# A two-layer decoder trunk: all of x loaded ahead of the weights, the first chunk reordered, the norms' transposes moved, and a bank of its own for the last 256 columns

## The chip, the cores and the metric

The kernel runs on one core of one Trainium2 chip. The metric is the device time of one execution in microseconds (us). Engine names are those of the profile: PE multiplies matrices, PEld is its weight load, DVE and ACT work element by element, POOL is a further element engine that also issues some DMAs, SP issues most DMAs. A number behind an `L` is a line of the kernel's source.

## The reference, cut to what matters

The trunk has two layers on 256 tokens of width 1024. Each layer is a half-step feed-forward network, a token mixer, and another half-step feed-forward network, each behind an RMS norm; a last RMS norm ends it.

```python
def rms_norm(x, w):
    y = xf * lax.rsqrt(jnp.mean(xf * xf, axis=-1, keepdims=True) + EPS)
    return (y * w)
def swiglu(x, w_in, w_out):
    gate, up = jnp.split(x @ w_in, 2, axis=-1)
    return (jax.nn.silu(gate) * up) @ w_out

for l in range(2):
    h = h + 0.5 * swiglu(rms_norm(h, ffn1_norm[l]), ffn1_w_in[l], ffn1_w_out[l])
    u = rms_norm(h, mix_norm[l])
    ... = jnp.split(u @ w_in[l], split_points, axis=-1)
    y_s = mamba2_branch(...); y_d = deltanet_branch(...)
    merged = sigmoid(gate_s) * (y_s @ ssm_w_branch[l]) + sigmoid(gate_d) * (y_d @ dn_w_branch[l])
    h = h + merged @ w_out[l]
    h = h + 0.5 * swiglu(rms_norm(h, ffn2_norm[l]), ffn2_w_in[l], ffn2_w_out[l])
return rms_norm(h, final_norm)
```

All inputs are float32.

## The kernel before

**Tiles and precision.** The 256 tokens are two token tiles of 128 (`t` = 0, 1). The stream `h` stays in SBUF as 128 x 2 x 1024. The weights come as a stream of 128 x 1024 tiles (`wraw`, 512 KB each), loaded by SP in the order of use (`load`, L157), five at a time. `prep` (L173) splits each into a high half `whi` (ACT, L67) and a low half `wlo` (DVE, L70); up to five split tiles exist. Activations are split in the same way, and each product is three matmuls: high x high, high x low weight, low x high (`mm3`, L315).

**Order of issue.** The program is written in one order, and a scheduler orders each engine's instructions from that; `tc.issue_after(ins)` puts an instruction behind another one, and `tc.high_priority` puts some ahead. Per tile index, `state["behind"]` names instructions that a split goes behind, and `state["late"]` one that only its low half goes behind. `take` (L201) hands the next split tile to a chunk and issues loads and splits ahead of it.

**Norms.** `norm_in` (L288) works tile by tile. For a token tile, `rstd_of` (L260) takes two square sums of 512 columns on ACT (`junk`), adds them on DVE (`zz`, L78), and takes the power of minus one half on POOL (`rsqrt`, L208). `rms_chain` (L271) then multiplies on DVE (`hn`, two halves of 512 columns), transposes each half on PE with four 128 x 128 transposes into a bank `hnT` (L281), and splits the bank into `uW`, high by ACT and low by DVE. There are five such norms between stages, and a sixth at the start, where `h` is x itself and the norm vector is spread by two matmuls from one row (`nw`, L245).

**The first chunk behind a norm.** `tok_chunk` (L329) multiplies four weight tiles (two 128-row slices each) by token tile 0, 24 matmuls of 512 columns, and then by token tile 1. PE does tile 0 while the norm of tile 1 is still under way on ACT, DVE and POOL; the transposes of tile 1 stand after 18 matmuls, with one matmul between their two groups. In a feed-forward network the next chunks are `fc` (`chan_chunk`, L346); in the mixer they are `z` chunks, and the mixer's small weights `wsr` are loaded, split into `wsc` (L561 to 564), and used behind the second `z` chunk.

**Start.** SP issues the norm row, token tile 0 of x, the identity (part of `cs`), four weight tiles, then token tile 1 of x (L221 to 230).

**End.** The last chunk of the last feed-forward network (`out_chunks` with `split`, L366) ends with 15 matmuls of 512 columns for token tile 1. `add` (L389) puts them on `h`, and L1248 to 1258 take the last norm, scale two halves of 512 columns, and SP issues two output DMAs per token tile.

## Time and profile before

| | us |
|---|---|
| median of 3 runs (lowest, highest) | 1547.75 (1547.63, 1549.64) |
| the profiled execution's own time | 1548.12 |
| its span, first instruction to last | 1546.4 |
| PE busy in the span | 1525.9 |
| DVE, ACT, POOL busy | 1228.8, 949.3, 86.9 |

A row of the timeline reads: start in us, duration in us, engine, line, operation, what is written `<-` what is read, the matmul's array shape, shape and type, the number of instructions merged; in brackets the idle time of the engine ahead of it and what ended it. A row of the waits reads: engine and what it waited with `<-` what it waited for, us in total, times, longest. A row of the windows reads: from:to, length, busy us and instructions of PE, PEld, DVE, ACT and POOL, PEclk, DMA busy share, GB/s. The end of a matmul is modelled: a 512-column matmul is shown with 0.39 us, while in an unbroken run the next one starts 0.23 us after it.

### The profile page before, as it was taken

Reading aid. Unit: us, or ns where it says so; the run is one execution under the profiler, and the core shown is the slowest. Engines: PE = TensorE matmul, PEld = TensorE weight load, DVE = VectorE, ACT = ScalarE, POOL = GpSimd, SP = SyncE. Lnnn points to the kernel's source line nnn. Section 1 sums busy time; section 2 is a strip of 40 time slices with the busy share of each in tenths; the row PEclk is TensorE's granted clock in tenths of the full one; section 3 lists DMA queues with packets and bytes.
Section 4 is the critical chain, followed back from the end, with each engine's and each line's share of the span. In section 5 each row is a group of like instructions: output and inputs, shape, how many; then the busy total and the mean of one; then the engine's idle time right before and its main releaser. Section 6 shows DMA issues by size and latency. Waiting matters only on the chain.

```text
span 1546.4 us, 29049 instructions
## 1 busy us (share of the span) xinstructions
PE 1525.9 (99%) x11458; PEld 1383.8 (89%) x11458; DVE 1228.8 (79%) x1856; ACT 949.3 (61%) x1534; POOL 86.9 (6%) x92
## 2 busy tenths in 40 slices
PE   8999999999999999999999999999999999999998
PEld 7999879999888888999899998899998888889996
DVE  6878769967899766788778887789579996678886
ACT  5655667765665645565555566676756665455564
POOL 0000110000000000000100012010000000000010
PEclk9999999999999999999999999999999999999999
DMA  7677765553465455577866687565345555556775
GB/s 273 193 265 228 226 223 169 185 164 110 177 209 172 158 170 192 185 248 214 266 220 226 204 253 236 183 196 184 117 138 203 178 168 184 177 178 190 248 240 156
DMA packets 98831, 305.73 MB, mean 198 GB/s; under 512 B 22837, under 2 KB 23813, under 8 KB 97670
## 3 DMA queue, kind: packets, MB, share of 16 engines
q1 hardware_dynamic: 94086, 291.29, 55.9%
q0 software_dynamic: 4608, 12.58, 4.9%
q8 instruction: 90, 1.47, 0.4%
q14 instruction: 47, 0.39, 0.1%
HBM read 297.72 MB, written 1.92 MB: 194 GB/s over the span
## 4 chain that ended last, share of the span: by engine, by line
PE 86%; DVE 5%; issue 3%; ACT 3%; DMA 2%; POOL 1%; POOLq 0%; SPq 0%; ACTq 0%; DVEq 0%
PE fc L327 9%; PE fc L321 9%; PE fc L326 9%; PE o L318 3%; PE o L317 3%; PE o L316 3%; PE t L316 3%; PE t L317 3%; PE t L318 3%; PE b L318 3%; PE b L316 3%; PE b L317 3%; PE p L317 2%; PE p L316 2%; PE p L318 2%
## 5 line engine op out<-in xcount | busy, mean ns | idle before, releaser
L70 DVE TENSOR_TENSOR wlo<-wraw,whi 128x1024 fp32r<-128x1024 f32 x488 | 592.2, 1221 | 188.1 <-ACT whi L67 174.5
L67 ACT ACTIVATE whi<-wraw 128x1024 fp32r<-128x1024 f32 x488 | 511.6, 1059 | 268.1 <-PE fc L326 91.6
L327 PE MATMUL fc<-uW,wlo 128*128 128x256 f32 x1280 | 354.8, 277 | 0.0
L321 PE MATMUL fc<-uW,whi 128*128 128x256 f32 x1280 | 354.0, 277 | 0.0
L326 PE MATMUL fc<-uW,whi 128*128 128x256 f32 x1260 | 348.2, 276 | 0.0
L321 PEld LDWEIGHTS fc<-uW,whi 128*128 128x128 f32 x1280 | 240.4, 188 | 0.8
L327 PEld LDWEIGHTS fc<-uW,wlo 128*128 128x128 f32 x1280 | 240.6, 188 | 0.0
L326 PEld LDWEIGHTS fc<-uW,whi 128*128 128x128 f32 x1260 | 236.5, 188 | 0.8
L67 ACT ACTIVATE whi<-wsum 128x1024 fp32r<-128x1024 f32 x64 | 68.0, 1062 | 58.8 <-PE fc L326 32.7
L316 PE MATMUL t<-whi,uW 128*128 128x512 f32 x256 | 101.9, 399 | 0.0
L317 PE MATMUL t<-wlo,uW 128*128 128x512 f32 x256 | 100.9, 394 | 0.2 <-DVE wlo L70 0.2
L318 PE MATMUL t<-whi,uW 128*128 128x512 f32 x256 | 100.5, 392 | 0.0
L70 DVE TENSOR_TENSOR wlo<-wsum,whi 128x1024 fp32r<-128x1024 f32 x64 | 78.2, 1222 | 7.9 <-ACT whi L67 5.6
L316 PE MATMUL b<-whi,bh 128*128 128x512 f32 x192 | 76.1, 398 | 0.3 <-ACT bh L67 0.2
L317 PE MATMUL b<-wlo,bh 128*128 128x512 f32 x192 | 74.9, 390 | 0.0
L318 PE MATMUL b<-whi,bl 128*128 128x512 f32 x192 | 74.3, 394 | 0.3 <-DVE bl L70 0.3
L321 PE MATMUL xs<-uW,whi 128*128 128x256 f32 x256 | 72.8, 285 | 0.0
L327 PE MATMUL xs<-uW,wlo 128*128 128x256 f32 x256 | 71.4, 279 | 0.0
L326 PE MATMUL xs<-uW,whi 128*128 128x256 f32 x254 | 70.6, 278 | 0.0
L316 PE MATMUL o<-whi,gh 128*128 128x512 f32 x160 | 62.5, 391 | 0.0
L318 PE MATMUL o<-whi,gl 128*128 128x512 f32 x160 | 62.3, 389 | 0.0
L317 PE MATMUL o<-wlo,gh 128*128 128x512 f32 x160 | 62.3, 389 | 0.0
(332 smaller groups left out, 3401.3 us busy)
## 6 DMA issues: line engine op xcount, KB each, us to landing
wraw<-in_wst_dram SPq DMA_DIRECT2D x504, 512.0 KB, 5.0
wsum<-in_wst_dram SPq DMA_DIRECT2D x16, 512.0 KB, 7.0
wsum<-in_wst_dram POOLq DMA_DIRECT2D x16, 512.0 KB, 8.2
dc<-rdram SPq DMA_DIRECT2D x8, 1024.0 KB, 8.1
nw<-in_norms_dram SPq DMA_DIRECT2D x6, 512.0 KB, 7.5
h<-u POOLq DMA_DIRECT2D x12, 256.0 KB, 6.3
gb<-rdram SPq DMA_DIRECT2D x8, 256.0 KB, 6.0
h<-in_x_dram SPq DMA_DIRECT2D x4, 256.0 KB, 5.6
```

The lines of the kernel that those rows point to most:

```text
L67: return A.activation(out=o, in_=i, func=func, **kw)
L70: return V.tensor_tensor(out=o, in0=a, in1=b, op=op)
L316: PE.matmul(ps, lh, rh, start=start, stop=False)
L317: PE.matmul(ps, lh, rl, start=False, stop=False)
L318: return PE.matmul(ps, ll, rh, start=False, stop=stop)
L321: PE.matmul(ps, wh, mh, start=start, stop=False)
L326: PE.matmul(ps, wh, ml, start=False, stop=False)
L327: PE.matmul(ps, wl, mh, start=False, stop=stop)
```

## The change

- **x first.** SP issues all four DMAs of x ahead of the weights. The norm row and the identity are issued by ACT.
- **First norm and first chunk** (`norm_first`, new). The norm chains of both token tiles come ahead of the first weight split's low half; only the first bank of each tile is transposed ahead of the chunk, the second banks after 9 and 12 of its matmuls as written. `tok_chunk` takes each weight tile for both token tiles before the next one.
- **The five norms.** For token tile 1 the transposes are written into `tok_chunk` after matmuls 18 and 20 (`TURN`); the low half of tile n+3 goes behind the `hn` of tile 1, the split of n+4 behind its transposes; the last two slices of token tile 0 are multiplied high x high, low x high, then high x low weight.
- **The mixer's small weights.** The split of `wsc` is written behind the first `z` chunk.
- **The end.** For token tile 1 the last 512 columns are multiplied as twice 256, the second 256 into a bank of their own (`tail`); the square sums, the addition and the product with the norm vector follow these pieces; the last output DMA is issued by ACT.

```diff
+TURN = (17, 19)
...
-        ahead("prepped", min(j + 1 if state["hold"] else j + NSPL, n_forms), prep)
+        ahead("prepped", min(j + 1 if state["hold"] else j + NSPL, n_forms, state["cap"]), prep)
...
-    nc.sync.dma_start(row[:], norms[0:1, :])
+    nc.scalar.dma_start(row[:], norms[0:1, :])
+    nc.scalar.dma_start(cs[:, 0:P], cst[:, 0:P])
     for t in range(2):
         for n in range(2):
             nc.sync.dma_start(
                 h[:, t, n * 512 : (n + 1) * 512], x[t * P : (t + 1) * P, n * 512 : (n + 1) * 512]
             )
-        if t == 0:
-            nc.sync.dma_start(cs[:, 0:P], cst[:, 0:P])
-            ahead("loaded", 4, load)
+    ahead("loaded", 4, load)
...
+    def norm_first(nw):
+
+        place_input()
+        with tc.high_priority(offset=PRI):
+            _, turn0 = rms_chain(0, nw)
+            ins, turn1 = rms_chain(1, nw)
+            state["behind"][0], state["late"][0] = [state["square"].ins], ins
+            ahead("prepped", 1, prep)
+            with tc.issue_after(state["whi"].ins):
+                first = turn0(0)
+            with tc.issue_after(first[0].ins):
+                done = turn1(0)
+        for i in range(1, 4):
+            state["behind"][i] = [done[0].ins]
+            state["late"][i] = done[1]
+        state["turns"] = {8: (turn0, 1), 11: (turn1, 1)}
+        state["first_chunk"] = True
...
                 state["behind"][n + 4] = (state["square"].ins, ins.ins)
                 state["late"][n + 2] = added
-                state["input"] = done
+                state["late"][n + 3] = ins
+                state["turns"] = {i: (turn, n_) for n_, i in enumerate(TURN)}
+                state["cap"] = n + 4
...
+        order = [(t, k0, w) for t in range(2) for k0, w in ws]
+        if first:
+            order.sort(key=lambda o: o[1])
+        i = 0
+        for t, k0, (wh, wl) in order:
+            three = []
+            for k in range(2):
+                uh, ul = (u[:, k0 + k, t * P : (t + 1) * P] for u in (uTh, uTl))
+                high, low = (w[:, k * 512 : (k + 1) * 512] for w in (wh, wl))
+                three.append([(uh, high), (uh, low), (ul, high)])
+            if t == 0 and len(ws) == 4 and k0 == (0 if first else KT - 2):
+                three = [[m[j] for m in three] for j in ((0, 1, 2) if first else (0, 2, 1))]
+            three = sum(three, [])
+            for j, (st, mv) in enumerate(three):
+                ins = PE.matmul(ps[t][:], st, mv, start=k0 == 0 and j == 0, stop=k0 == KT - 2 and j == 5)
+                if i in state["turns"]:
+                    turn, n = state["turns"].pop(i)
+                    with tc.high_priority(offset=PRI), tc.issue_after(ins.ins):
+                        state["input"] = turn(n)
+                    if not state["turns"] and state["cap"] < n_forms:
+                        state["late"][state["cap"]] = state["input"][1]
+                        state["cap"] = n_forms
+                i += 1
...
+                if t == 1 and split:
+                    order = [o for o in order if o[1] == 0]
+                    order += [(k, 1, c, c + 256) for c in (0, 256) for k in range(len(kk))]
...
+                    if c0:
+                        begin, bank = k == kk[0], ps[2][:, 0:256]
...
+            if nw is None and t == 1:
+                banks.append((po[2][:, 0:256], 768))
...
         z_unit(0, None)
-
+        wsc = cpool.tile([P, KT, 2, 48], F32R, tag="wsc", name="wsc")
+        with tc.issue_after(state["input"][0].ins), tc.issue_after(state["input"][1].ins):
+            act(wsc[:, :, 0], wsr[:])
+            tt(wsc[:, :, 1], wsr[:], f(wsc[:, :, 0]), ALU.subtract)
...
+        cuts = ((0, 512), (512, 1024)) if t == 0 else ((0, 512), (512, 768), (768, 1024))
...
+        nc.sync.dma_start(out[t * P : (t + 1) * P, 0:512], o[0][:])
+        (nc.scalar if t else nc.sync).dma_start(out[t * P : (t + 1) * P, 512:1024], o[1][:])
```

What the change moves on the engines, at three places.

ACT at the start, before, from the second square sum of token tile 0 on; `uW_108` is the transposed input, of token tile 0 in the first pair and of tile 1 in the second, `hnT_...` the four banks, `junk` the square sums:

```order
L67 ACTIVATE junk_112,ss_109<-h_78 128x512
L67 ACTIVATE whi_135<-wraw_85 128x1024
L67 ACTIVATE uW_108<-hnT_121 128x4x128
L67 ACTIVATE uW_108<-hnT_128 128x4x128
L67 ACTIVATE whi_139<-wraw_87 128x1024
L67 ACTIVATE whi_193<-wraw_89 128x1024
L67 ACTIVATE junk_144,ss_143<-h_78 128x512
L67 ACTIVATE junk_146,ss_143<-h_78 128x512
L67 ACTIVATE whi_197<-wraw_91 128x1024
L67 ACTIVATE uW_108<-hnT_155 128x4x128
L67 ACTIVATE uW_108<-hnT_162 128x4x128
```

and with the change, where the first two `uW` rows are the first banks of tile 0 and tile 1, and the later two the second banks:

```order
L68 ACTIVATE junk_112,ss_109<-h_78 128x512
L68 ACTIVATE junk_122,ss_121<-h_78 128x512
L68 ACTIVATE junk_124,ss_121<-h_78 128x512
L68 ACTIVATE whi_133<-wraw_87 128x1024
L68 ACTIVATE uW_108<-hnT_137 128x4x128
L68 ACTIVATE uW_108<-hnT_144 128x4x128
L68 ACTIVATE whi_175<-wraw_89 128x1024
L68 ACTIVATE whi_179<-wraw_91 128x1024
L68 ACTIVATE whi_183<-wraw_93 128x1024
L68 ACTIVATE uW_108<-hnT_218 128x4x128
L68 ACTIVATE whi_187<-wraw_165 128x1024
L68 ACTIVATE uW_108<-hnT_228 128x4x128
```

The square sums of tile 1 moved ahead of the first weight split, and the last bank of tile 1 now stands behind the split of the fifth weight tile (`whi_187`).

DVE at the second norm, before, from the square sums of token tile 1 (`zz_6809`) to the end of its input; `wlo_6851` is the low half of tile n+3 and `wlo_6855` that of n+4:

```order
L78 TENSOR_SCALAR zz_6809<-ss_6804 128x1
L70 TENSOR_TENSOR wlo_6851<-wraw_6692,whi_6850 128x1024
L73 SCALAR_TENSOR_TENSOR hn_6812<-h_78,zz_6809,nw_2185 128x512
L73 SCALAR_TENSOR_TENSOR hn_6814<-h_78,zz_6809,nw_2185 128x512
L70 TENSOR_TENSOR wlo_6855<-wraw_6694,whi_6854 128x1024
L70 TENSOR_TENSOR uW_108<-hnT_6816,uW_108 128x4x128
L70 TENSOR_TENSOR uW_108<-hnT_6823,uW_108 128x4x128
```

and with the change:

```order
L79 TENSOR_SCALAR zz_6809<-ss_6804 128x1
L74 SCALAR_TENSOR_TENSOR hn_6812<-h_78,zz_6809,nw_2171 128x512
L74 SCALAR_TENSOR_TENSOR hn_6814<-h_78,zz_6809,nw_2171 128x512
L71 TENSOR_TENSOR wlo_6837<-wraw_6692,whi_6836 128x1024
L71 TENSOR_TENSOR uW_108<-hnT_6864,uW_108 128x4x128
L71 TENSOR_TENSOR uW_108<-hnT_6873,uW_108 128x4x128
L71 TENSOR_TENSOR wlo_6919<-wraw_6694,whi_6918 128x1024
```

Each of the two low halves moved back by one step: n+3 behind `hn`, n+4 behind `uW`.

ACT in the first mixer, before, from the input of token tile 1 on; `yz` is the output of the first `z` chunk for a token tile, `whi_2215` the split of tile n+5, the second tile of the next chunk:

```order
L67 ACTIVATE uW_108<-hnT_2178 128x4x128
L67 ACT_TABLE_LOAD
L67 ACTIVATE ea_2379<-rp_2189 128x40
L67 ACT_TABLE_LOAD
L67 ACTIVATE yz_2196<-t0_2197 128x512
L67 ACTIVATE wsc_2193<-wsr_2191 128x8x48
L67 ACTIVATE whi_2215<-wraw_2051 128x1024
L67 ACTIVATE whi_2221<-wraw_2053 128x1024
```

and with the change, where `whi_2304` is the same split:

```order
L68 ACTIVATE uW_108<-hnT_2225 128x4x128
L68 ACTIVATE yz_2179<-t0_2180 128x512
L68 ACTIVATE whi_2304<-wraw_2051 128x1024
L68 ACTIVATE wsc_2262<-wsr_2177 128x8x48
L68 ACTIVATE whi_2308<-wraw_2053 128x1024
L68 ACT_TABLE_LOAD
L68 ACTIVATE ea_2379<-rp_2175 128x40
L68 ACTIVATE whi_2312<-wraw_2055 128x1024
L68 ACT_TABLE_LOAD
```

The split of tile n+5 moved ahead of `wsc`, and the two table loads with `ea` behind it.

More of the change, by code (lines that the diff above doesn't have):

```diff
@@ L147, in trunk_kernel @@
     n_forms = len(plan)
-    state = {"loaded": 0, "prepped": 0, "taken": 0, "last": None, "hold": False, "behind": {}, "late": {}, "first": 0}
+    state = {"loaded": 0, "prepped": 0, "taken": 0, "last": None, "hold": False, "behind": {}, "late": {}, "first": 0, "turns": {}, "first_chunk": False, "cap": n_forms}
     raws, halves = {}, {}
@@ L560, in mixer @@
             nc.sync.dma_start(wsr[:], wsm[l])
-        wsc = cpool.tile([P, KT, 2, 48], F32R, tag="wsc", name="wsc")
-        with tc.issue_after(state["input"][0].ins), tc.issue_after(state["input"][1].ins):
-            act(wsc[:, :, 0], wsr[:])
-            tt(wsc[:, :, 1], wsr[:], f(wsc[:, :, 0]), ALU.subtract)
         snw = lp[:, 240:256]
```

93 lines of the change are left out of this document (43 added, 50 removed).

## Prediction

> **What bounds the kernel now.** I read the busy shares first, then PE's waits, then PE's stretch at each place that the diff touches.
>
> ```profile
> PE 1525.9 (99%) x11458; PEld 1383.8 (89%) x11458; DVE 1228.8 (79%) x1856; ACT 949.3 (61%) x1534; POOL 86.9 (6%) x92
> ...
> PE hnT L281 <- DVE hn L73: 3.6, 7, 0.9
> PE cbb L1006 <- DVE vb L70: 2.9, 2, 1.6
> ...
> PE t L317 <- DVE wlo L70: 0.2, 1, 0.2
> ```
>
> PE, the matmul engine, is busy 99% of the span, and no matmul is taken away. So only time in which PE stands still can be won: at the start, at the five norms between stages, at the end. The wait rows (us in total, times, longest) put the largest group there: the transposes `hnT` wait seven times for `hn`, twice at the start and once at each of the five norms. The waits inside the mixers (`cbb` and others) are not touched; they are for chains that start from PE's own earlier products and so move with PE. What PE gains at one of these places therefore arrives at the end.
>
> **The five norms.** Token tile 0 is normalised while PE is still at the stage before. Tile 1 is normalised while PE multiplies tile 0. The rows are those of the second norm; first DVE and POOL for tile 0, then the same chain for tile 1, then PE.
>
> ```profile
> 592.22 0.21 DVE L78 TENSOR_SCALAR zz<-ss 128x1 f32<-128x1 f32 x1 [0.79 <-ACT junk L67]
> 592.51 0.56 POOL L209 TENSOR_TENSOR zz<-zz,mhalf 128x1 f32<-128x1 f32 x1 [61.43 <-DVE zz L78]
> 593.10 1.41 DVE L73 SCALAR_TENSOR_TENSOR hn<-h,zz,nw 128x512 f32<-128x512 f32 x2 [0.67 <-POOL zz L209]
> ...
> 600.24 0.21 DVE L78 TENSOR_SCALAR zz<-ss 128x1 f32<-128x1 f32 x1
> 600.36 1.21 DVE L70 TENSOR_TENSOR wlo<-wraw,whi 128x1024 fp32r<-128x1024 f32 x1
> 600.52 1.47 POOL L209 TENSOR_TENSOR zz<-zz,mhalf 128x1 f32<-128x1 f32 x1 [7.45 <-DVE zz L78]
> 602.03 1.41 DVE L73 SCALAR_TENSOR_TENSOR hn<-h,zz,nw 128x512 f32<-128x512 f32 x2 [0.46 <-POOL zz L209]
> ...
> 602.15 0.39 PE L318 MATMUL f<-whi,uW 128*128 128x512 f32 x1
> 602.93 0.63 PE L281 MATMUL hnT<-cs,hn 128*128 128x128 f32 x4 [0.39 <-DVE hn L73]
> ...
> 186.18 0.40 PE L318 MATMUL o<-whi,gl 128*128 128x512 f32 x1
> 186.42 1.04 PE L281 MATMUL hnT<-cs,hn 128*128 128x128 f32 x8
> ```
>
> From `zz` to `hn` it is 0.88 us for tile 0 and 1.79 us for tile 1. The difference is the power on POOL: 0.56 us alone, 1.47 us while DVE runs a weight split (`wlo`) beside it. The change puts that split behind `hn`, so I expect 0.88 us again: `hn` at 601.12 instead of 602.03, its first half by 601.87. PE reaches the transposes 0.24 us after its last matmul began (186.18 to 186.42, where nothing is missing), at 602.39, and no longer waits. Before, 0.78 us lay there, so 0.54 us go. The waits at all five are alike:
>
> ```profile
> PE hnT L281 <- DVE hn L73: 1.9, 5, 0.4
> ```
>
> (1.9 us, because the view lets a matmul end after 0.39 us while the next may start after 0.23.) From start to start the five gaps are 0.74 and four times 0.77 to 0.78; less 0.24 each, **2.65 us** in all.
>
> What is late next? The split that moved now runs at 602.5 to 603.7. Its low half is wanted by the last two matmuls of tile 0, since the change orders the last pair high, high, then low activations, then low weights. These come after the two groups of transposes (0.4 us each) and four matmuls, at 604.2: 0.5 us to spare. The subtractions that complete tile 1's input end near 604.3 and 605.1; the first is wanted at 605.1 and the second 2.8 us later. On SP the norm vector `nw` now stands one weight load earlier and that load follows `hn`, for a weight that is wanted several tiles later. If the moved split came late after all, each norm would lose what it gained, 0.5 us.
>
> **The mixer's small weights.** In the first mixer ACT waited for the DMA of `wsr`, with the next weight splits queued behind it, and PE then waited for the split of the second tile of its next chunk.
>
> ```profile
> 201.70 0.53 ACT L67 ACTIVATE wsc<-wsr 128x384 fp32r<-128x384 f32 x1 [1.55 <-DMA wsr<-in_wsm_dram]
> ...
> 203.88 0.40 PE L316 MATMUL t<-whi,uW 128*128 128x512 f32 x1
> 204.48 0.50 PE L317 MATMUL t<-wlo,uW 128*128 128x512 f32 x1 [0.20 <-DVE wlo L70]
> ```
>
> The gap is 0.60 us where 0.23 is normal. In the new order one more split stands ahead of `wsc`, just the one that was missing. The two table loads and `ea` also go behind it. ACT will still wait for `wsr`, but PE then works on tiles that are ready: **0.37 us**, in the first mixer only; the second shows no such gap.
>
> **The start.** First the bounds, then the sum.
>
> ```profile
> 3.92 0.63 ACT L67 ACTIVATE junk<-h 128x512 f32<-128x512 f32 x1 [1.90 <-DMA h<-in_x_dram]
> 6.20 1.41 DVE L73 SCALAR_TENSOR_TENSOR hn<-h,zz,nw 128x512 f32<-128x512 f32 x2 [0.67 <-POOL zz L209]
> 7.00 1.97 PE L281 MATMUL hnT<-cs,hn 128*128 128x128 f32 x8 [0.93 <-DVE hn L73]
> 7.84 1.06 ACT L67 ACTIVATE whi<-wraw 128x1024 fp32r<-128x1024 f32 x1 [2.56 <-DMA wraw<-in_wst_dram]
> 9.44 0.79 PE L316 MATMUL f<-whi,uW 128*128 128x512 f32 x1 [0.47 <-ACT uW L67]
> ...
> 13.12 0.45 PE L317 MATMUL f<-wlo,uW 128*128 128x512 f32 x1
> 13.40 0.40 PE L318 MATMUL f<-whi,uW 128*128 128x512 f32 x1
> ...
> 16.45 0.63 PE L281 MATMUL hnT<-cs,hn 128*128 128x128 f32 x4 [0.81 <-DVE hn L73]
> ...
> 18.28 1.05 ACT L67 ACTIVATE whi<-wraw 128x1024 fp32r<-128x1024 f32 x1
> ...
> 24.64 0.28 PE L321 MATMUL fc<-uW,whi 128*128 128x256 f32 x1
> ...
> 4.00:5.00 1.00, 1.00 (x2) 0.33 (x1) 0.00 (x0) 1.00 (x3) 0.00 (x0) 1.00 0.62 154
> 6.00:8.00 2.00, 1.07 (x6) 1.00 (x6) 1.41 (x2) 0.16 (x1) 0.16 (x1) 1.00 1.03 373
> 8.00:10.00 2.00, 1.53 (x6) 0.85 (x4) 1.07 (x1) 2.00 (x4) 0.00 (x0) 1.00 0.91 294
> 12.00:14.00 2.00, 2.00 (x8) 1.57 (x7) 1.62 (x2) 1.09 (x4) 0.00 (x0) 1.00 1.04 416
> ```
>
> Before, the first weight is split at 7.84, the first matmul starts at 9.44, PE stands still ahead of 16.45 for tile 1, and the chunk is over when `fc` begins at 24.64. Now the second half of x, 0.52 MB, goes ahead of the weights. At 373 GB/s that is 1.4 us. Against it, x is issued 0.41 us earlier (ACT issues the norm row and the identity), and the stretch from 4 to 5 us, in which the DMA engines moved only 154 GB/s, is filled, which is worth 0.6 us. So the first weight comes 0.4 to 0.5 us later; I take 8.3. Its bounds are 0.2 us later (all at 416 GB/s) and 3.0 us later (the 0.52 MB at 154 GB/s less the earlier issue); the latter would end at 1545.6. The two issues cost ACT between nothing and 0.8 us (SP's take 0.35 and 0.43); ACT then loads a table of 1.28 us and still waits for x, so I take nothing.
>
> Tile 0's `hn` comes about 0.3 us earlier, 5.9 to 7.3, tile 1's at 8.2 to 9.6. Its first half is there at 8.9 and PE turns it by 9.9 (eight transposes took 1.97). ACT has split the weight by 9.3 and made tile 0's input by 9.9. So the first matmul starts at 9.9, 0.45 us later than before.
>
> From there I see no wait. Two token tiles use a weight in 12 matmuls, so the four weights are wanted at about 9.9, 15, 18 and 20.5; x and all four are 3.2 MB, which at 294 to 416 GB/s have landed by 14. With 48 matmuls and two groups of four transposes: half speed lasts 3.8 us from the first matmul, as before (9.44 to about 13.2, matmuls 0.43 us apart, then 0.23), so 9 matmuls in 3.9 us, 39 in 9.0, the groups 0.5 each. `fc` begins at 23.8, **0.9 us** earlier.
>
> The Trainium skill, "TensorE: Matmul & The Clock Gate", Part 1, says that the array starts at half its clock and is released after one busy window of about 3.4 us, and that the windows run free of the kernel's start. The rows agree with the two speeds; the profile's PEclk column shows 1.00 throughout and cannot show the gate. By that rule the release may fall anywhere from 3.4 to 6.8 us after the first matmul; on average that is 1.3 us later than here, by estimate 0.6 us more time, so 1543.7.
>
> **The end.**
>
> ```profile
> 1539.64 0.69 DVE L73 SCALAR_TENSOR_TENSOR h<-o,h 128x512 f32<-128x512 f32 x1 [1.98 <-PE o L318]
> 1540.37 0.63 ACT L67 ACTIVATE junk<-h 128x512 f32<-128x512 f32 x1 [2.67 <-DVE h L73]
> ...
> 1541.12 0.21 DVE L78 TENSOR_SCALAR zz<-ss 128x1 f32<-128x1 f32 x1
> ...
> 1542.06 0.72 ACT L67 ACTIVATE fo<-fo,zz 128x512 f32<-128x512 f32 x1 [0.97 <-POOL zz L209]
> ...
> 1542.58 0.81 SPq L1258 DMA_DIRECT2D out_dram<-fo  x2
> ...
> 20.65 0.39 ACT L67 ACTIVATE sg<-f 128x256 f32<-128x256 f32 x1
> 21.07 0.42 DVE L70 TENSOR_TENSOR sg<-sg,f 128x256 f32<-128x256 f32 x1 [0.47 <-ACT sg L67]
> ```
>
> Behind the last matmul stand an addition, a square sum, the root, a scaling and two output DMAs. With 256 columns the addition takes 0.42 instead of 0.69 and the square 0.39 instead of 0.63: 0.5 us. The second output was issued by SP 0.41 us behind the first, at 1542.98; ACT can now issue it as soon as its own scaling ends, 0.2 us earlier: **0.7 us**. PE's 15 matmuls of 512 columns become 30 of 256. In `fc` these start 0.11 us apart with a weight load each, so both forms take 3.4 us; if each took the 0.19 us of its weight load, it would be 5.7. I take 3.4.
>
> **Sum.** 2.65 + 0.37 + 0.9 + 0.7 = 4.6 us off the profiled execution's 1548.12, which is 0.37 above the median of the runs shown. Off the median 1547.75: **1543.1 us**, 0.30% faster. A measurement of this kernel can tell about 0.2%, 3.1 us, from no change.
>
> **Rivals.**
> - *The clock is released twice as late*, 7.7 us after the first matmul. For: the time of release rests on one trace. Another 3.8 us at 0.43 instead of 0.23 cost 1.8 us: 1544.9. Released at once: 9 matmuls at 0.20 less, 1541.3.
> - *The norms do not gain*, because POOL takes 1.47 us for another reason than the split beside it, so the change does not do what it is arranged for. Against: in the start and for tile 0 the power takes 0.56. The 2.65 are missing: 1545.8.
> - *Slower: ACT's queue.* In the new order ACT splits the fifth weight ahead of making the second half of tile 1's input. PE wants that input at 19.7, so the fifth weight must land by 18.0. With it and ahead of it are 4.65 MB, and 2.1 us go by beside the moving (3.92 less 1.15 less 0.26 MB at 373 GB/s): at 294 to 416 GB/s it lands by 14.0 to 18.7. At 200 GB/s, towards the 154 of the poor stretch, it lands at 26.1, PE stands 8.1 us, and the time is 1551.2. From 22.6 on (235 GB/s) the change loses. Against: before, a weight with as many bytes ahead was split at 18.28 without waiting.
>
> **How the numbers follow.** The forecast has 0.61, the clock released at once 0.06, released late 0.16, norms without gain 0.14, slower 0.03. The range takes in all but the last and some unforeseen sum of them: 1541.3 to 1546.0. Faster by over 0.2% (below 1544.65) are the forecast, the early clock and the third of the late ones that costs under 1.5 us: 0.72; slower 0.03; within 0.2% the rest, 0.25.
>
> **What would show it.** At the norms the power on POOL at 0.56 for tile 1 and PE's waits for `hn` gone; no PE gap behind `wsc`; `fc` beginning near 23.8; zz 0.95 us behind the last addition's start instead of 1.48. I am wrong if PE waits anew: for a low half at the end of tile 0, for tile 1's input at the start, or between the halved matmuls of the end.

## The result, and the profile after

| | before | changed kernel |
|---|---|---|
| median (lowest, highest), 11 runs each | 1547.75 us (1546.39, 1550.19) | 1543.89 us (1543.02, 1546.71) |
| the profiled execution's own time, its span | 1548.12, 1546.4 | 1543.84, 1542.1 |

The ratio of the changed kernel to the one before is 0.9977, with a 95% interval of 0.9969 to 0.9985: 0.23% faster. The forecast was 1543.1 us, in a range of 1541.3 to 1546.0. The total came within 0.8 us of the forecast, but its terms did not come as forecast: the start and the end gave less, and in the profiled pair the mixers gave more, by luck, as shown below.

Three views of the changed kernel first: the page's busy times, PE's waits (us in total, times, longest), and the rows of the second norm for token tile 1, on DVE, POOL and PE.

```profile
PE 1525.1 (99%) x11473; PEld 1385.3 (90%) x11473; DVE 1229.8 (80%) x1859; ACT 949.8 (62%) x1536; POOL 82.6 (5%) x92
```

```profile
PE hnT L282 <- DVE hn L74: 2.5, 2, 1.4
...
PE cbb L1045 <- DVE vb L71: 1.3, 2, 0.9
...
PE pst L664 <- ACT smT L68: 0.5, 1, 0.5
```

```profile
598.94 0.21 DVE L79 TENSOR_SCALAR zz<-ss 128x1 f32<-128x1 f32 x1
...
599.24 0.56 POOL L210 TENSOR_TENSOR zz<-zz,mhalf 128x1 f32<-128x1 f32 x1 [7.46 <-DVE zz L79]
...
599.83 1.42 DVE L74 SCALAR_TENSOR_TENSOR hn<-h,zz,nw 128x512 f32<-128x512 f32 x2 [0.67 <-POOL zz L210]
...
600.84 0.39 PE L366 MATMUL f<-whi,uW 128*128 128x512 f32 x1
601.07 0.60 PE L282 MATMUL hnT<-cs,hn 128*128 128x128 f32 x4
```

PE is again busy 99% of the span, and still the span is 4.3 us shorter: 3.5 us of that is PE's idle time (20.5 us before, 17.0 now), and 0.8 us is time shown as busy, with the modelled ends. The seven waits for `hn` are two, both in the start. The power takes 0.56 us instead of 1.47, `hn` follows `zz` by 0.89 us, and the transposes begin 0.23 us after a matmul, without a wait. The wait of `t` for `wlo` (0.2) is gone as well. New is a wait of `pst`, and the waits of `cbb`, which the change does not touch, fell from 2.9 to 1.3 us.

Where the 4.3 us lie is read from rows that both programs have: the begin of `fc` behind the first chunk, and then POOL's power for token tile 1 (`599.24` above is the one of norm 2). N1 to N5 are the five norms, "last" is the norm at the end. All in us; a cell is the time between two such rows.

| profile | fc begins | N1 to N2 (mixer 1) | N2 to N3 | N3 to N4 | N4 to N5 (mixer 2) | N5 to last | last to end of span |
|---|---|---|---|---|---|---|---|
| before | 24.64 | 408.07 | 178.20 | 178.06 | 407.95 | 176.75 | 4.92 |
| changed | 24.92 | 406.50 | 177.62 | 177.45 | 406.82 | 176.05 | 4.92 |
| difference | +0.28 | -1.57 | -0.58 | -0.61 | -1.13 | -0.70 | 0.00 |

The two stretches without a mixer and without an end show a norm alone: 0.58 and 0.61 us.

The start of the changed kernel, on ACT, DVE and PE:

```profile
5.21 0.63 ACT L68 ACTIVATE junk<-h 128x512 f32<-128x512 f32 x1 [1.05 <-DMA h<-in_x_dram]
...
6.85 1.41 DVE L74 SCALAR_TENSOR_TENSOR hn<-h,zz,nw 128x512 f32<-128x512 f32 x2 [0.67 <-POOL zz L210]
...
9.05 1.41 DVE L74 SCALAR_TENSOR_TENSOR hn<-h,zz,nw 128x512 f32<-128x512 f32 x2 [0.67 <-POOL zz L210]
9.10 1.06 ACT L68 ACTIVATE whi<-wraw 128x1024 fp32r<-128x1024 f32 x1 [1.36 <-DMA wraw<-in_wst_dram]
```

```profile
9.85 1.11 PE L282 MATMUL hnT<-cs,hn 128*128 128x128 f32 x4 [1.09 <-DVE hn L74]
10.70 1.75 PE L366 MATMUL f<-whi,uW 128*128 128x512 f32 x3
...
15.23 0.69 PE L282 MATMUL hnT<-cs,hn 128*128 128x128 f32 x4
...
24.92 0.28 PE L340 MATMUL fc<-uW,whi 128*128 128x256 f32 x1
```

The second half of tile 0 of x is squared at 5.21, where it was 4.56 before; `hn` of tile 0 starts at 6.85 (forecast 5.9), that of tile 1 at 9.05 (8.2), the first matmul at 10.70 (9.9). The first ten matmuls take 4.53 us.

The end of the changed kernel:

```profile
1535.15 0.28 PE L337 MATMUL tail<-whi,gl 128*128 128x256 f32 x1
1535.27 0.28 PE L335 MATMUL tail<-whi,gh 128*128 128x256 f32 x1
...
1535.82 0.42 DVE L74 SCALAR_TENSOR_TENSOR h<-tail,h 128x256 f32<-128x256 f32 x1 [0.37 <-PE tail L337]
...
1536.82 0.21 DVE L79 TENSOR_SCALAR zz<-ssf 128x1 f32<-128x1 f32 x1
```

`zz` follows the last addition's start by 1.00 us (1.48 before). The 256-column matmuls start 0.12 us apart, 3.6 us for thirty. From the last addition to the end of the span it is 6.28 us (6.76 before).

### The profile page after: what moved, and what is told of

The parts are those of the page before. It is cut to its first block, busy times and chain, and to the rows that moved or that the text cites. A ratio compares the mean times of both kernels' runs of the same rounds, so it can differ in the third digit from the quotient of the medians.

```text
span 1542.1 us, 29082 instructions
## 1 busy us (share of the span) xinstructions
PE 1525.1 (99%) x11473; PEld 1385.3 (90%) x11473; DVE 1229.8 (80%) x1859; ACT 949.8 (62%) x1536; POOL 82.6 (5%) x92
## 3 DMA queue, kind: packets, MB, share of 16 engines
q8 instruction: 90, 1.47, 0.4%
## 4 chain that ended last, share of the span: by engine, by line
PE 90%; DVE 3%; ACT 3%; DMA 2%; issue 1%; POOL 0%; SPq 0%; POOLq 0%; ACTq 0%; DVEq 0%
PE fc L346 10%; PE fc L340 9%; PE fc L345 9%; PE t L366 9%; PE o L337 4%; PE o L336 4%; PE o L335 4%; PE f L366 3%; PE b L337 3%; PE b L335 3%; PE b L336 3%; PE p L336 2%; PE p L335 2%; PE p L337 2%; PE xs L340 1%; PE xs L345 1%
## 5 line engine op out<-in xcount | busy, mean ns | idle before, releaser
L366 PE MATMUL t<-whi,uW 128*128 128x512 f32 x512 | 165.4, 397 | 0.0
L366 PEld LDWEIGHTS t<-whi,uW 128*128 128x128 f32 x512 | 95.9, 188 | 21.6 <-issue 1.3
L335 PE MATMUL o<-whi,gh 128*128 128x512 f32 (+1 forms) x160 | 62.0, 388 | 0.0
L337 PE MATMUL o<-whi,gl 128*128 128x512 f32 (+1 forms) x160 | 61.8, 386 | 0.0
L336 PE MATMUL o<-wlo,gh 128*128 128x512 f32 (+1 forms) x160 | 61.7, 386 | 0.0
```

What stands on the lines that cost most here:

```text
L335: PE.matmul(ps, lh, rh, start=start, stop=False)
L336: PE.matmul(ps, lh, rl, start=False, stop=False)
L337: return PE.matmul(ps, ll, rh, start=False, stop=stop)
L366: ins = PE.matmul(ps[t][:], st, mv, start=k0 == 0 and j == 0, stop=k0 == KT - 2 and j == 5)
```

## The experiments

### One line undone at the norms (late_split)

```diff
-                state["late"][n + 3] = ins
```

> The changed kernel, with one line undone: the low half of weight tile n+3 no longer goes behind the hn of token tile 1, so DVE runs it between zz and hn again. Theory (POOL's power is slowed by the weight split beside it): the power takes 1.40 to 1.47 us for tile 1 at all five norms instead of 0.56, PE waits for hn five times by about 0.4 us, each norm is 0.5 us longer, and the time is 1546.5 us (1543.9 and 2.65). Rival (the power is slow for another reason, or PE's wait is taken over by something else): the power stays at 0.56, or PE's rows at the norms stay as they are; 1543.9. The scheduler also moves table loads on ACT in the mixer, so norms 3 and 5, with no mixer behind them, are the clean ones.

Measured: 1546.48 us median, 0.9994 of the kernel before (0.9985 to 1.0003). The second norm in this run, on DVE, POOL and PE, and its row of PE's waits:

```profile
598.79 1.22 DVE L71 TENSOR_TENSOR wlo<-wraw,whi 128x1024 fp32r<-128x1024 f32 x1
598.96 1.47 POOL L210 TENSOR_TENSOR zz<-zz,mhalf 128x1 f32<-128x1 f32 x1 [7.45 <-DVE zz L79]
...
601.36 0.63 PE L282 MATMUL hnT<-cs,hn 128*128 128x128 f32 x4 [0.39 <-DVE hn L74]
```

```profile
PE hnT L282 <- DVE hn L74: 4.3, 7, 1.3
```

With the split beside it the power takes 1.39 to 1.47 us at all five norms again, and the five waits are back. N2 to N3 takes 178.19 us, 0.57 more than in the changed kernel, and N3 to N4 177.86, 0.41 more. (N5 to last is 1.67 longer; 0.8 of that is a wait of `o` for a `wlo` that the changed kernel's profile does not have.) The theory holds. The Trainium skill, "SBUF — State Buffer", § Who interferes with whom, says that a DVE instruction with two inputs in SBUF contends with a GpSimd instruction that reads SBUF, since both read through a shared port; `wlo` is such an instruction, and 1.47 against 0.56 us agrees.

### That line alone in the kernel before (norm_line)

```diff
                 state["late"][n + 2] = added
+                state["late"][n + 3] = ins
```

> The kernel before, with one line of the change alone: the low half of weight tile n+3 goes behind the hn of token tile 1 at the five norms (the scheduler then also puts one weight split ahead of the mixer's small ones). Transposes and the order of the matmuls stay as before. Theory (the power beside the split is what costs, and the new order of the last matmuls of tile 0 only keeps the moved split off the path): the power takes 0.56 us at all five, PE's five waits of 0.4 for hn go, but PE now asks for the low half one or two matmuls after the transposes and waits for it, 0 to 0.6 us per norm; time between 1545.1 (all five gains kept) and 1547.7 (all lost again). Rival (the gain comes from where the transposes stand): the waits for hn stay, 1547.7.

Measured: 1548.39 us, 1.0005 (0.9997 to 1.0014): nothing gained, and not for the reason that I expected. The third norm in this run (POOL, DVE, PE); behind it the kernel before at the same place:

```profile
779.61 0.55 POOL L209 TENSOR_TENSOR zz<-zz,mhalf 128x1 f32<-128x1 f32 x1 [7.51 <-DVE zz L78]
...
780.20 1.41 DVE L73 SCALAR_TENSOR_TENSOR hn<-h,zz,nw 128x512 f32<-128x512 f32 x2 [0.73 <-POOL zz L209]
781.00 1.32 PE L281 MATMUL hnT<-cs,hn 128*128 128x128 f32 x8 [0.41 <-DVE hn L73]
```

```profile
780.15 1.42 DVE L73 SCALAR_TENSOR_TENSOR hn<-h,zz,nw 128x512 f32<-128x512 f32 x2 [0.44 <-POOL zz L209]
...
780.96 0.66 PE L281 MATMUL hnT<-cs,hn 128*128 128x128 f32 x4 [0.39 <-DVE hn L73]
```

The power takes 0.55 us and `hn` follows it at once, 0.84 us sooner after the power's start than before. But PE waits 0.41 us for it as it did: the scheduler, which orders by its own estimates, puts the transposes sooner too, three matmuls behind the power's start and not seven. So PE reaches them just as early as `hn` came earlier. N2 to N3 takes 178.24 us, as before. The gain needs both edits: the split behind `hn`, and the transposes written at a fixed place behind matmuls 18 and 20 (`TURN`). Neither alone gives any of it. The new order of the last matmuls of token tile 0 was not run alone.

### The old start (old_start)

```diff
-    nc.scalar.dma_start(row[:], norms[0:1, :])
-    nc.scalar.dma_start(cs[:, 0:P], cst[:, 0:P])
+    nc.sync.dma_start(row[:], norms[0:1, :])
...
+        if t == 0:
+            nc.sync.dma_start(cs[:, 0:P], cst[:, 0:P])
+            ahead("loaded", 4, load)
...
-        state["turns"] = {8: (turn0, 1), 11: (turn1, 1)}
-        state["first_chunk"] = True
```

> The changed kernel with the whole start as before: the old order of the DMAs, the old first norm, and the first chunk one token tile after the other. Theory (the new start gains nothing, because the first weight's split comes 1.26 us later and that eats the wait for tile 1 that was saved): fc begins at 24.6 us as before instead of 24.9, and the time is 1543.6. Rival (the profiled run of the changed kernel was unlucky in its clock, and the new start is worth the forecast 0.9 on average): the time is 1544.8, and fc here begins later than in the median run of the changed kernel.

Measured: 1545.05 us, 0.9982 (0.9973 to 0.9991); `fc` begins at 25.09. That is 0.25 us above the rival's 1544.8 and 1.45 above the theory's 1543.6. It is 1.2 us above the changed kernel's median, with intervals that overlap. One profile is no measure of a start. The same old start has `fc` at 24.64, 25.09 and 25.24 in three profiles (before, this one, norm_line), mean 24.99; the new one at 24.92, 24.10, 25.32, 24.17 and 24.55 in five (changed, late_split, mixer_waits, wsr_early, dc_high), mean 24.61. So the new start is worth 0.4 us on average, which is not clear of the scatter (0.6 us among the three, 1.2 among the five). The profiled pair, with +0.28, sets the earliest `fc` of the old start against the second latest of the new one.

### The norm row and the identity on SP again (rings)

```diff
-    nc.scalar.dma_start(row[:], norms[0:1, :])
-    nc.scalar.dma_start(cs[:, 0:P], cst[:, 0:P])
+    nc.sync.dma_start(row[:], norms[0:1, :])
...
+        if t == 0:
+            nc.sync.dma_start(cs[:, 0:P], cst[:, 0:P])
...
-        (nc.scalar if t else nc.sync).dma_start(out[...], o[1][:])
+        nc.sync.dma_start(out[...], o[1][:])
```

> The changed kernel with the norm row and the identity issued by SP again (row ahead of x, identity between its two token tiles; x still ahead of the weights), and the last output DMA issued by SP. Theory for the start (the transfers issued by ACT ran beside x and held its second half back, 5.2 us instead of 4.5): the second half of tile 0 is squared near 4.5, hn of tile 0 begins near 6.2 instead of 6.85, and fc near 24.4. Rival (what holds x back is what SP issues behind it, tile 1 of x and the first weight): hn of tile 0 stays at 6.7 to 6.9, fc at 24.9 or later. For the end: if the issue by ACT was worth its 0.2 us, the span ends 6.5 us behind the last addition instead of 6.3; if the two output transfers only slow each other, it stays at 6.3.

Measured: one run, 1549.04 us. ACT's row of tile 0's second half, and DVE's of `hn`, tile 0 and tile 1:

```profile
4.77 0.62 ACT L68 ACTIVATE junk<-h 128x512 f32<-128x512 f32 x1
...
6.39 1.41 DVE L74 SCALAR_TENSOR_TENSOR hn<-h,zz,nw 128x512 f32<-128x512 f32 x2 [0.67 <-POOL zz L210]
...
10.30 1.41 DVE L74 SCALAR_TENSOR_TENSOR hn<-h,zz,nw 128x512 f32<-128x512 f32 x2 [0.67 <-POOL zz L210]
```

Tile 0 came as the theory said (second half at 4.77, `hn` at 6.39). But tile 1's `hn` came at 10.30 instead of 9.05, the first matmul at 12.34, and `fc` at 26.61: the forecast of 24.4 missed, since it looked at one tile only. In the eight profiles with the changed kernel's transfers tile 0's `hn` begins at 6.41 to 7.17 and tile 1's at 8.90 to 9.63. So the 6.39 here is within 0.02 us of their scatter, and only the loss at tile 1 is clear of it: in this one profile the two small transfers on SP cost tile 1 at least 0.67 us, and what they gain at tile 0 is not shown. The Trainium skill, "DMA: Bandwidth & Descriptors", § Issuing engines are not separate DMA queues, says that transfers issued by several engines run on the same 16 DMA engines and interleave, and that only issue time is saved. Tile 0's 6.85 in the changed kernel beside 6.39 here would agree, but may be scatter.

At the end the rival holds: from the last addition to the end of the span it is 6.27 us with both output DMAs on SP and 6.28 with one on ACT (6.21 to 6.29 in the nine others). The two transfers end together whichever engine issues the second.

### The identity made on the chip (ident_pool)

```diff
-    nc.scalar.dma_start(cs[:, 0:P], cst[:, 0:P])
...
+    G.memset(ident, 0.0)
+    G.affine_select(out=ident, in_=ident, compare_op=ALU.not_equal, fill=1.0, base=0, pattern=[[-1, P]], channel_multiplier=1)
```

> The changed kernel with the 64 KB of the identity (128 rows of 512 bytes) not loaded: POOL makes it in place by a memset and a select while x is on its way. Theory (these short rows hold the DMA engines up at the start, since the slow stretch came right behind them, at 4 to 5 us before and in the run with SP's queue): x lands sooner, the second half of tile 0 is squared at 4.4 to 4.8 instead of 5.2, the first weight is split by 8.5 instead of 9.1, fc begins 0.5 to 0.8 us earlier than in the changed kernel, and the time is 1543.2. Rival (the slow stretch belongs to x's own transfers or to their start): no row of the start moves by more than 0.2 us, 1543.9.

Measured: 1545.91 us, 0.9988 (0.9979 to 0.9996). The theory falls. Two of the four squares of x on ACT, the second and the last:

```profile
5.01 0.63 ACT L68 ACTIVATE junk<-h 128x512 f32<-128x512 f32 x1 [0.50 <-DMA h<-in_x_dram]
...
8.20 0.63 ACT L68 ACTIVATE junk<-h 128x512 f32<-128x512 f32 x1 [1.82 <-DMA h<-in_x_dram]
```

Tile 0 is 0.2 us sooner, but x's last quarter is squared at 8.20 (7.02 in the changed kernel) and `fc` begins at 25.91. In uw_first, below, whose transfers are those of the changed kernel, it is 7.99. So the landing of that quarter differs by 1 us between runs of one list of transfers, and weights that are issued behind x are in flight with it. What decides it stays open.

### Matmuls that keep PE busy (warm)

```diff
+    wm = slots.tile([P, 512], F32R, tag="y1", name="wm")
+    V.memset(f(wm[:]), 1.0)
+    wb = accb("warm")
+    def warm(n, ins=None):
...
+                ins = PE.matmul(wb[:], wm[:, 0:P], wm[:], start=True, stop=True)
+    warm(3)
...
+    warm(3, ins)
...
                 first = turn0(0)
+                warm(3, state["tr"])
```

> The changed kernel with nine matmuls more, 128x512 on a tile of ones into a bank that nothing reads: three ahead of the norm row's matmuls, three behind them, three between the first transposes of token tiles 0 and 1. Theory (PE runs at half speed until it has been busy for a while without a gap, and the idle time ahead of the first chunk is what delays the release): the first chunk runs at 0.23 us per matmul from its first one, fc begins near 22.9 instead of 24.9, and the time is 1541.9. Rival 1 (the release is tied to the time since the kernel's start): the chunk's first ten matmuls stay 0.43 apart, fc at 24.9, 1543.9. Rival 2 (the added matmuls stand in the way): the first transposes come later than 7.65 and the time is 1544.4.

Measured: 1543.91 us, 0.9979 (0.9969 to 0.9988), so no gain in time. PE's first transposes, the chunk's first matmul, and the transposes behind its tenth:

```profile
8.35 1.05 PE L295 MATMUL hnT<-cs,hn 128*128 128x128 f32 x4
...
10.97 0.71 PE L380 MATMUL f<-whi,uW 128*128 128x512 f32 x2
...
13.91 0.27 PE L295 MATMUL hnT<-cs,hn 128*128 128x128 f32 x1
```

The first ten matmuls take 2.94 us here, against 4.53, 4.04, 4.61, 3.64 and 4.35 in the five profiles with the new start. The trace's record of the granted clock begins where the half speed ends: here at 10.75 us, 0.22 ahead of the chunk's first matmul, and in the five others 2.5 to 5.0 us behind it. In best and uw_first below, with seven added matmuls, it is 1.0 and 0.8 us behind it. So PE's earlier work does decide when it is released, and rival 1 falls. Rival 2 holds as well: the first transposes stand behind the added matmuls until 8.35 instead of 7.65. `fc` begins at 23.51, 1.1 us ahead of the others' mean, but N1 to N2 took 407.89 us in this run, 1.4 more than in the changed kernel's profile.

### Two instructions moved in the mixers (mixer_waits), and dc's loads raised (dc_high)

How PE's `cbb` waits, first in the kernel before and then in the changed one, in the first mixer:

```profile
404.66 2.29 DVE L70 TENSOR_TENSOR dc<-dc,ac 128x2048 f32<-128x2048 f32 x1 [1.81 <-DMA dc<-rdram]
...
407.61 0.70 PE L1006 MATMUL cbb<-BC 128*128 128x256 f32 x2 [1.63 <-DVE vb L70]
```

```profile
403.38 2.29 DVE L71 TENSOR_TENSOR dc<-dc,ac 128x2048 f32<-128x2048 f32 x1 [0.64 <-DMA dc<-rdram]
...
406.33 0.70 PE L1045 MATMUL cbb<-BC 128*128 128x256 f32 x2 [0.46 <-DVE vb L71]
```

DVE stands in line behind `dc`, which waits for a DMA, and PE waits for `vb` behind it. Both kernels have this; only the landing differs.

```diff
-                    tt(ov, ob[:], os_[:], ALU.add)
+                    state["ov"] = tt(ov, ob[:], os_[:], ALU.add)
...
+            with tc.issue_after(state["ov"].ins):
+                tt(dc[:], dc[:], ...)
...
+            if name == "s" and state["cap"] < n_forms:
+                state["behind"][state["cap"]] = [state["smT"].ins]
```

> The changed kernel with two instructions moved in the mixers: DVE's subtraction on dc, which waits for a DMA, goes behind the addition vb that PE's cbb needs; and the third of three weight splits on ACT goes behind smT, for which PE's pst waits. Theory (the mixers' waits of PE hang on DMA landings and on ACT's queue, not only on PE's earlier products, and differ from run to run for that reason): cbb waits 0.5 us or less in all instead of 1.3 to 2.4, pst does not wait, and the time is 1542.0 (about 1.3 and 0.6 us less). Rival (the chains behind move along and PE waits a little later for the same things, xsb or the b matmuls): those rows grow by as much, 1543.9.

Measured: 1554.76 us, 1.0045 (1.0033 to 1.0057). The waits of `cbb` and `pst` are gone from PE's list, as the theory says, but at its head stands a new one:

```profile
PE yT L1170 <- DVE og L74: 5.7, 2, 2.9
```

The other experiment left DVE's order to the scheduler and only raised the DMAs:

```diff
+            with tc.high_priority(offset=PRI):
                 nc.sync.dma_start(
                     dc[:].rearrange("p h t l -> p (h t l)"),
```

> The changed kernel with the loads of dc raised in the scheduler: on SP the first two stand one weight load earlier, the third nine earlier; the scheduler moves some xsb transposes and weight splits of that part along. Theory (cbb waits for dc's landing through DVE's queue: its wait is that of DVE for dc less 0.2 us in every profile): one weight load of 0.5 MB less in front is 1.2 to 1.4 us, dc waits under 0.4 us, cbb at most 0.2 in all instead of 1.3 to 2.4; the time is 1542.4 if nothing else moves. Rival (what the scheduler moves along costs as much, as with the two instructions moved before): other waits (yT, b, xsb) grow by over 1 us and the time is 1543.9 or more.

Measured: 1551.75 us, 1.0026 (1.0016 to 1.0035). Here `cbb` did not even gain:

```profile
PE cbb L1045 <- DVE vb L71: 3.0, 2, 1.9
...
PE yT L1170 <- DVE og L74: 2.5, 2, 1.3
```

PE's wait for `smT` at `pst` also grew here, to 2.1 us in all, 1.8 at most. In both runs N1 to N2 takes 411.5 us and N4 to N5 412.3, against a mean of 407.5 in five other profiles (changed, old_start, rings, warm, ident_pool). The moves reorder the instructions that follow on ACT, DVE and PE, and PE then waits longer in one piece. That costs twice, because PE's clock is halved behind such a wait. In mixer_waits, first mixer, PE's wait and then a row of the windows, whose third number from the end is the granted clock:

```profile
463.50 1.11 PE L1170 MATMUL yT<-cs,yz 128*128 128x128 f32 x4 [2.88 <-DVE og L74]
```

```profile
463.06:469.89 6.83, 5.50 (x14) 4.18 (x15) 6.31 (x11) 3.40 (x7) 0.50 (x1) 0.50 0.50 157
```

The clock is 0.50 for 6.83 us there and again from 1231.06 on. In dc_high it is 0.50 for 3.41 us three times: from 212.59 on, behind 1.76 us of waiting at `pst`; from 1175.15 on, behind 1.88 at `cbb`; and from 1233.17 on, behind 1.25 at `yT` and 1.35 at `b`. No other profile has such a stretch between the start and the end of PE's work. At half clock 3.41 us of work take 1.7 us too long, so by estimate the clock is 1.7 and 3.4 of dc_high's 4.0 and 4.8 us, and about 2.6 and 2.8 of the 4.1 and 4.8 in mixer_waits (half of the 4.39 and 5.60 us of its `b` matmuls there, and 0.45 of a slow `yT` in the first mixer). The rest is the waits themselves; they were not taken apart further.

### The small weights issued earlier (wsr_early)

```diff
-            wsr = s2.tile([P, KT, 48], F32, tag="s2", name="wsr")
-            nc.sync.dma_start(wsr[:], wsm[l])
...
+        with tc.issue_after(state["last"].ins):
+            wsr = s2.tile([P, KT, 48], F32, tag="s2", name="wsr")
+            nc.sync.dma_start(wsr[:], wsm[l])
         mixer(l, norm_vec(3 * l + 2), wsr)
```

> The changed kernel with one DMA moved on SP: the mixer's small weights wsr are issued ahead of the norm vector nw, of lp and of rp, not behind them. SP's nw waits for the last hn of the norm, so that wsr now leaves SP before it. The orders of ACT, DVE and PE stay. Theory (the wait of PE's pst, which came new with the change, is set by the landing of wsr: over the profiles it is the wait of wsc for wsr less 2.0 us): wsc waits under 1.5 us in both mixers, pst waits in neither, N1 to N2 (the power of token tile 1, norm 1 to norm 2) takes 406.8 us instead of a mean of 407.5, and the time is 1543.0. Rival (ACT's own queue, with three weight splits ahead of smT, sets it): pst keeps its 0.5 to 1.5 us in the first mixer, 1543.9.

Measured: 1543.22 us, 0.9969 (0.9958 to 0.9981). First the changed kernel in its first mixer (SP, ACT, PE), then this one:

```profile
194.77 0.33 SPq L215 DMA_DIRECT2D nw<-in_norms_dram  x1
...
195.68 0.38 SPq L600 DMA_DIRECT2D wsr<-in_wsm_dram  x1
...
201.84 0.53 ACT L68 ACTIVATE wsc<-wsr 128x384 fp32r<-128x384 f32 x1 [2.42 <-DMA wsr<-in_wsm_dram]
...
210.88 0.38 PE L664 MATMUL pst<-cs,smT 96*128 96x96 f32 x2 [0.46 <-ACT smT L68]
```

```profile
192.31 0.42 SPq L1284 DMA_DIRECT2D wsr<-in_wsm_dram  x1
...
196.27 0.53 ACT L68 ACTIVATE wsc<-wsr 128x384 fp32r<-128x384 f32 x1 [0.26 <-DMA wsr<-in_wsm_dram]
...
209.17 0.38 ACT L68 ACTIVATE smT<-psm 96x256 f32<-96x256 f32 x1 [0.78 <-PE psm L657]
...
209.66 0.33 PE L662 MATMUL pst<-cs,smT 96*128 96x96 f32 x2
```

`nw` waits on SP for the last `hn`, and `wsr` stood behind it. Issued 3.4 us sooner, it lands 5.6 us sooner, ACT then waits for PE at `smT` and not the other way round, and `pst` waits in neither mixer. The theory holds for the wait. Of the stretches, N4 to N5 fell to 406.18, N1 to N2 did not (407.43, where 406.8 was expected): beyond PE's listed waits a mixer scatters by about half a microsecond from run to run, and I could not say where.

### Both together (best), and ACT's order at the start turned (uw_first)

best is wsr_early with seven added matmuls (two, two and three, where warm has three at each place).

> The changed kernel with wsr issued ahead of nw, and with seven added matmuls on a tile of ones whose result nothing reads: two ahead of the norm row's matmuls, two behind them, three between the first transposes of the two token tiles; fewer ahead, so that the transposes are not held up. Theory: the transposes of tile 0 at 7.5 instead of 8.35 in the run with nine, the clock released by 12, fc at 23.0 instead of 23.5 (24.1 to 25.3 without), with wsr 1542.0. Rival (what the start gains is lost again in the mixers, which wait for DMA landings): fc at 23.0 all the same, but N1 to N2 and N4 to N5 over 407.5 and the time 1543.5 or more.

Measured: 1542.47 us, 0.9965 (0.9952 to 0.9977), the lowest median of all; its interval lies below 1 and overlaps that of the changed kernel. Tile 0's transposes begin at 7.80, the half speed ends at 11.77, and `fc` begins at 23.36, where 7.5, 12 and 23.0 were expected. N1 to N2 takes 407.86 us and N4 to N5 406.04, so the rival is met in one mixer and not in the other. uw_first is best with this edit:

```diff
-            state["behind"][0], state["late"][0] = [state["square"].ins], ins
-            ahead("prepped", 1, prep)
-            with tc.issue_after(state["whi"].ins):
-                first = turn0(0)
-                warm(3, state["tr"])
+            first = turn0(0)
+            warm(3, state["tr"])
+            state["behind"][0], state["late"][0] = [first[0].ins], ins
+            ahead("prepped", 1, prep)
```

> The kernel of the run before (wsr ahead of nw, seven added matmuls) with ACT's order at the start turned: the first part of token tile 0's input, uW, is made ahead of the first weight's split, not behind it. Theory (the first matmul is late because uW stands behind the split, which waits for the first weight's DMA until about 9.1): with the split at 9.1 to 9.2, the first matmul starts near 10.2 instead of 10.77, fc near 22.8 instead of 23.4, and the time is 1541.9. Rival (tile 1's transposes, queued on PE ahead of the first matmul, set its start): first matmul at 10.6 or later, 1542.5. The scheduler also puts the second banks' uW behind the fifth weight's split; if that weight lands after 14, PE waits for them ahead of the third weight's matmuls, and fc begins at 23.4 or later.

Measured: 1542.62 us, 0.9965 (0.9951 to 0.9979). PE's rows, first of best, then of uw_first with ACT's row of `uW`:

```profile
10.00 1.12 PE L295 MATMUL hnT<-cs,hn 128*128 128x128 f32 x4
10.77 1.53 PE L380 MATMUL f<-whi,uW 128*128 128x512 f32 x3
```

```profile
8.75 0.60 ACT L68 ACTIVATE uW<-hnT 128x512 fp32r<-128x512 f32 x1
...
10.43 1.11 PE L295 MATMUL hnT<-cs,hn 128*128 128x128 f32 x4 [0.43 <-DVE hn L74]
11.20 1.54 PE L379 MATMUL f<-whi,uW 128*128 128x512 f32 x3
```

The rival holds. `uW` was ready by 9.35, and the first matmul did not come earlier: it starts 0.77 us behind the transposes of tile 1 in both runs, and 0.85 in the changed kernel. Tile 1's `hn`, so x's landing, sets it.

## Why the prediction was right in the sum and wrong in its parts

| step | forecast | measured |
|---|---|---|
| five norms | -2.65 | -2.95 (0.58 and 0.61 at the two that stand alone) |
| mixer's small weights | -0.37 | +0.1: the old wait gone, a new one of 0.5 in its place |
| mixers' other waits | 0 | -1.6 in the profiled pair (`cbb`), by the landing of a DMA |
| start | -0.9 | +0.28 in the profiled pair, -0.4 over eight profiles, not clear of their scatter |
| end | -0.7 | -0.3 from the last chunk on, and 0.2 lost ahead of it in the last network |

**The five norms** were right, mechanism and place, and 0.06 us per norm too small. late_split shows the cause. What the prediction did not say is that the gain hangs on the transposes' fixed place as well, as norm_line shows. The rival "the norms do not gain" is out, and the moved split did not come late.

**The mixer's small weights** failed at the step "PE then works on tiles that are ready". The gap behind the low half closed. But `smT` stands behind three weight splits on ACT, and these behind `wsc`: in all eight mixers of these profiles in which `wsc` waited over 2.3 us for its DMA, PE waited at `pst`, from 0.5 at 2.4 to 1.8 at 3.7, which is about the wait less 2.0 (mixer_waits aside, where `smT` was moved). wsr_early takes the cause away, and the wait goes. So the edit alone is worth about nothing on average: in the mean of the changed kernel, old_start, rings, warm and ident_pool, N1 to N2 takes 407.45 us and N4 to N5 407.46, 0.6 and 0.5 less than before (one profile), which is the norm. No run undoes this edit alone.

**The mixers' other waits** were said to move with PE, "for chains that start from PE's own earlier products". One of them runs through DVE's queue and a load from DRAM, and its wait differs from run to run: DVE's wait for `dc` is 0.5 to 2.2 us in these profiles, and PE's at `cbb` about 0.2 less. In the profiled pair that gave 1.6 of the 4.3 us. The change does not touch it, and its scatter covers the difference, so it was luck that it made up for what the start did not give. With the averages in place of the pair the terms add up to about -3.4 us (norms -2.95, start -0.4, end -0.1). The medians differ by 3.9, and by the interval 2.3 to 4.8; the forecast took 4.6.

**The start** failed in its first row: x was to come 0.3 us earlier because it was issued 0.41 us earlier, and the slow stretch was to be filled, for 0.6 us. The first half of tile 0 did come earlier (squared at 3.43, before at 3.92), but the second came later, and with it tile 0's `hn`, by 0.65 us (over profiles: mean 6.77 in eight with the new transfers; 6.20, 6.38 and 6.71 with the old start). What follows came as forecast from there: tile 1's `hn` 2.2 us behind it (forecast 2.3), the first matmul 0.85 behind the transposes, no wait in the chunk, so that the rival of ACT's queue did not occur. The first weight was split at 9.10, 0.8 later than taken but within its bounds. The clock's release was the second part. The ten matmuls took 3.64 to 4.61 us where the forecast has 4.1, so the size taken was near the middle; by the record of the clock the release came 2.5 to 5.0 us behind the first matmul, 3.9 on average, where 3.8 was taken from one trace. In the kernel before it was 3.8, with the same start in norm_line and old_start 6.1 and 6.2: part of the +0.28 is an early release in the one profile of before. The rival of a late release, 7.7 us after the first matmul, was not met; the longest, about 6 us, was in old_start and norm_line, with the old start. The Trainium skill, "TensorE: Matmul & The Clock Gate", Part 1, says that the windows run free of the kernel's start; five different values for one start agree. The prediction's 3.4 to 6.8 us behind the first matmul does not hold at its lower end, since 2.5 was met: in wsr_early the 3.41 us ahead of the release, from 10.01 on, begin with transposes. The prediction also held that the PEclk column cannot show the gate. It reads 1.00 at the start, where the record has not begun, but 0.50 in the mixers of mixer_waits and dc_high.

**The end** was right for the addition and the square (0.48 of 0.5). The thirty halved matmuls start 0.12 us apart and not 0.11 and cost 0.2 more than taken, and the DMA issued by ACT gained nothing, as rings shows.

## What to carry to other kernels

When a scheduler places instructions, an operand that comes earlier may only move the place where its reader waits; pin the reader too, and read the waits again. Ahead of a first transfer, ask what else is in flight on the same DMA engines, since an earlier issue is not an earlier landing. And where a wait hangs on a DMA's landing, take several profiles before you put its change down to an edit. Behind a new wait of the matmul engine read its granted clock too, since the wait can cost more than its own length.

## What the runs showed of the hardware that was not expected

- The clock seems to be decided in steps of 3.41 us. The half-clock stretches in the mixers last 3.41 or 6.83 us, and in mixer_waits the full clock ahead of the first and between the two lasts 447.15 and 761.17 us, which are 131 and 223 steps. Counted so, the steps in the mixers with 1.76 us or more of PE's idle time were followed by half clock, and those with up to 1.63 us were not. The 2.04 us wait of `cbb` in best fell into two steps, with 1.62 us in the longer part, and kept the clock.
- Counted in these steps, passes on a one-row operand do not lead to the release. In norm_line the step from 2.53 to 5.95 us, counted back from the release at 16.18, was filled by them (2.43 to 6.18), and the clock stayed at half until 16.18. In warm PE was occupied from 1.62 us on by added matmuls, these passes (3.78 us) and transposes. The step from 3.92 to 7.34 there was mostly such passes and brought no release; the one from 7.34 to 10.75, with full matmuls and transposes, did. So transposes did not prevent it.
- The scatter of about 3.7 us between runs of one program has at least three parts that the profiles show: the release (0.97 us between the fastest and the slowest ten matmuls of one start), the landing of x's last quarter (1 us) and DVE's wait for `dc` (0.5 to 2.2 us, so up to 1.7 per mixer).
